# Triangular blocks through DRAM in 1 KB pieces on two queues, and more rotary and scaling work on GpSimd, in a two-layer hybrid backbone step

## The chip, the core and the metric

The kernel runs on one core of one Trainium2 chip. The time is device microseconds (us) of one execution. Three runs of the kernel before took 1982.02, 1990.4 and 2092.3 us, a median of 1990.4 us.

## The reference, cut to what matters

The program is one step of a two-layer backbone for 128 context tokens and 512 latent tokens, of width 1024. Every layer adds a gated mixer and a gated feed-forward to `x`. The mixer has four head groups side by side: grouped-query attention (GQA) with rotary, neighbourhood attention, a bidirectional gated delta rule (DeltaNet), and latent attention (MLA). The change touches three of them. For each of the 10 chunks of 64 tokens, both directions and 4 heads, DeltaNet solves a unit-triangular system:

```python
    a = jnp.where(strict, jnp.einsum('nbhid,nbhjd->nbhij', kb, kc) * dmask, 0.0)
    sol = lax.linalg.triangular_solve(a + jnp.eye(c, dtype=jnp.float32), rhs,
                                      left_side=True, lower=True, unit_diagonal=True)
    u, w = sol[..., :dv], sol[..., dv:]
    def step(s, xs):
        v_new = u_i - jnp.einsum('bhcd,bhde->bhce', w_i, s)
        ...
        s = s * gl_i[..., None, None] + jnp.einsum('bhcd,bhce->bhde', kd_i, v_new)
```

GQA normalises queries and keys per head and rotates them (`x1 * cos - x2 * sin`, `x2 * cos + x1 * sin`); MLA normalises its compressed query and key-value rows by a factor per token.

## The kernel before

All 640 tokens are worked on together, in fp32; a matrix product is made of three matmuls, from a rounded high part and the rest of each weight (`weights`, L311 to L322: a DMA load, a ScalarE cast into `whi`, a VectorE subtraction into `wlo`).

**The order on TensorE is written out by a planner.** `_Order` (L190 to L273) runs generators, each with a rank; a generator says with `yield` from which planned time on it may go on, and the first ready one of the lowest rank issues its matmuls next. `od.via(("DVE", 1.6), ...)` returns when a chain of operations on the named engines would be done by the planner's own bookkeeping, and `od.now + 9.5` is a plain delay. The order is fixed when the kernel is built: at run time TensorE takes its instructions in that order and waits where an operand is not there. The instructions of the other engines are put in order by a scheduler that simulates time, except those in `in_turn` (L303), which keep the order in which the program names them.

**The DeltaNet chain** (`delta_chain`, L785) has the rank 0 and runs through both layers' mixers: features, chunk matrices `M` (L988), inverse of 16x16 diagonal blocks (`inverse16`, L1014), two levels of doubling to 64x64 (`inverse`, L1061), the scan over chunks (L1159) and the output (L1246). Beside it the planner fills TensorE with projections (`rest`, L1901, dense, rank 2), and in the first layer with the modulation's products (`trickle`, L1930).

**`inverse16` makes two trips through DRAM.** The scratch `dinv` (L434) has for each of two trips the layout row group `r`, direction `d`, block `b` (20), quarter `q` (4), 256 elements. Trip 1: eight DMAs on SP (L1025) scatter the 16x16 blocks of `M` in 64-byte pieces, then two DMAs (L1034, L1035) of 160 KB each read them back, one block row of 4 KB to a partition, 40 partitions each; a VectorE copy (L1037, `in_turn`) transposes the second direction, and 60 small VectorE instructions per layer eliminate (L1044, L1048). Trip 2: two DMAs of 160 KB write the result (L1051, and L1052 behind the copy L1050), eight (L1055) gather it into `rt`, and VectorE's block transposes (L1081, `in_turn`) feed the first matmuls of `inverse` (`invp`). The planner allows 9.5 us for trip 1 and 10.0 us for trip 2.

In `inverse`, `fourth` copies the diagonal blocks of `rt` into `M` on VectorE (L1128, four copies for each of three groups); the scan's `ysp` matmuls read `M`. `gqa_norm` (L1409) scales `ar` on VectorE (L1425), multiplies by the gain on GpSimd (L1427), makes the sine part `gsw` on GpSimd (L1439), and does the last two operations of the rotary, times cosine and plus `gsw`, on VectorE (L1441, L1442), for four of five tiles. `mla_norm` (L1525) loads a tile of latent rows `mcr` (one buffer), rotates 32 columns on GpSimd, scales the other columns on VectorE (L1552, `in_turn`), and TensorE transposes it (`mtp`). GpSimd also makes `kd` (L1187) and the scaled state (L1191) for each step of the scan.

Of the kernel before, what the change touches and what calls it, by code (L numbers as in the profile page):

```python
# [11 lines left out]
F32 = mybir.dt.float32  # L12
# [3 lines left out]
ALU = mybir.AluOpType  # L16
# [11 lines left out]
L = 2  # L28
# [259 lines left out]
class _Build:  # L288
# [97 lines left out]
    def setup(self):  # L386
        nc, A, ctx = self.nc, self.A, self.ctx
        cp = self.cp = ctx.enter_context(self.tc.tile_pool(name="const", bufs=1))
        self.wp = ctx.enter_context(self.tc.tile_pool(name="wts", bufs=1))
        self.dp = ctx.enter_context(self.tc.tile_pool(name="dram", bufs=1, space=DRAM))  # L390
        cT = cp.tile([128, KD, 2], F32, name="cT")
        nc.sync.dma_start(out=cT, in_=A["cT"])
        pc = cp.tile([128, A["pcol"].shape[1]], F32, name="pcol")
        nc.sync.dma_start(out=pc, in_=A["pcol"])
        cb = cp.tile([128, A["cbase"].shape[1]], F32, name="cbase")
        nc.sync.dma_start(out=cb, in_=A["cbase"])
        cst = _constants()
        off = 0
        for k in _CBASE:
            n = cst[k].reshape(128, -1).shape[1]  # L400
            v = cb[:, off:off + n]
            off += n
            sh = cst[k].shape[1:]
            if len(sh) == 2:
                v = v.rearrange("p (a b) -> p a b", a=sh[0])
            elif len(sh) == 3:
                v = v.rearrange("p (a b c) -> p a b c", a=sh[0], b=sh[1])
            setattr(self, k, v)
        self.ones = cp.tile([128, 128], F32, name="ones")
        nc.vector.memset(self.ones, 1.0)  # L410
        par, off = {}, 0
        for k, sh in _PAR.items():
            n = int(np.prod(sh))
            v = pc[:, off:off + n]
            off += n
            if len(sh) == 2:
                v = v.rearrange("p (a b) -> p a b", a=sh[0])
            elif len(sh) == 3:
                v = v.rearrange("p (a b c) -> p a b c", a=sh[0], b=sh[1])
            par[k] = v  # L420
        self.par = par
        self.sc = cp.tile([128, KD, 32], F32, name="sc")
        nc.vector.memset(self.sc, 0.0)
        nc.scalar.activation(self.sc[:, :, 0:2], cT, AF.Silu)
        self.mods = [cp.tile([128, 48, 2], F32, name=f"mods{l}") for l in range(L)]
        self.oms = [cp.tile([128, 2, KD, 2], F32, name=f"oms{l}") for l in range(L)]
        self.dscr = {
            "x": self.dp.tile([128, KD, T], F32, name="dx"),
            "x1": self.dp.tile([128, KD, T], F32, name="dx1"),
            "nat": self.dp.tile([L, 4, 128, T], F32, name="dnat"),  # L430
            "bv": self.dp.tile([L, T, 256], F32, name="dbv"),
            "craw": self.dp.tile([L, 128, 5, 416], F32, name="dcraw"),
            "lat": self.dp.tile([L, 4, 128, T], F32, name="dlat"),
            "inv": self.dp.tile([L, 2, 2, 2, 20, 4, 256], F32, name="dinv"),  # L434
        }


# [438 lines left out]
    def gates(self, l, gz, dn, dt, ps):  # L876

        nc, od = self.nc, self.od
# [22 lines left out]
        nc.vector.tensor_tensor(out=ld, in0=m[:, 0], in1=eb, op=ALU.mult)  # L901
        self.lf = small("lf")
        nc.vector.tensor_scalar(out=self.lf, in0=m[:, 1], scalar1=-1.0, scalar2=None, op0=ALU.mult)
        yield od.via(("DVE", 1.6), ("ACT", 2.2), ("DVE", 0.5)) + 4.0
        yield "dn", 1
        gp = ps.tile([128, 2, 2, 10, 2], F32, tag="dn", name="gp")
        for d in range(2):
# [106 lines left out]
    def inverse16(self, l, dt):  # L1014

        nc, od = self.nc, self.od
        Z = self.dscr["inv"][l]
        rt = dt.tile([128, 2, 20, 32], F32, name="rt")
        nc.gpsimd.memset(rt.rearrange("p d b c -> p (d b c)"), 0.0)
        M = self.M.rearrange("p d n q c -> p d (n q) c")  # L1020

        for r in range(2):
            for q in range(4):
                p = slice(64 * r + 16 * q, 64 * r + 16 * q + 16)
                nc.sync.dma_start(out=Z[0, r, :, :, q].rearrange("d b (j i) -> j (d b) i", j=16),  # L1025
                                  in_=M[p, :, :, 16 * q:16 * q + 16].rearrange("p d b i -> p (d b) i"))

        def t(name):
            return self.ta(dt, name, 1024).rearrange("p (q j i) -> p q j i", q=4, j=16)

        X, V, W = t("ivx"), t("ivv"), t("ivw")
        S = W
        nc.gpsimd.memset(X.rearrange("p q j i -> p (q j i)"), 0.0)
        nc.sync.dma_start(out=X[0:40].rearrange("p q j i -> p (q j i)"), in_=Z[0, :, 0].rearrange("r b q e -> r b (q e)"))  # L1034
        nc.sync.dma_start(out=S[64:104].rearrange("p q j i -> p (q j i)"), in_=Z[0, :, 1].rearrange("r b q e -> r b (q e)"))  # L1035
        yield od.now + 9.5
        self.in_turn(nc.vector.tensor_copy(X[64:104], S[64:104].rearrange("p q j i -> p q i j")))  # L1037
        nc.gpsimd.tensor_copy(V.rearrange("p q j i -> p q (j i)"), self.eye16.unsqueeze(1).to_broadcast([128, 4, 256]))
        p = slice(0, 104)
        for j in range(15):  # L1040
            sh = [104, 2, j + 1, 15 - j]
            qs = (slice(0, 2), slice(2, 4))
            for q in qs:
                nc.vector.tensor_tensor(out=W[p, q, 0:j + 1, 0:15 - j], in0=V[p, q, 0:j + 1, j:j + 1].to_broadcast(sh),  # L1044
                                        in1=X[p, q, j:j + 1, j + 1:16].to_broadcast(sh), op=ALU.mult)
            for q in qs:
                v = V[p, q, 0:j + 1, j + 1:16]
                nc.vector.tensor_tensor(out=v, in0=v, in1=W[p, q, 0:j + 1, 0:15 - j], op=ALU.subtract)  # L1048
        yield od.via(("DVE", 18.0)) + 4.0
        nc.vector.tensor_copy(S[64:104], V[64:104].rearrange("p q j i -> p q i j"))  # L1050
        nc.sync.dma_start(out=Z[1, :, 0].rearrange("r b q e -> r b (q e)"), in_=V[0:40].rearrange("p q j i -> p (q j i)"))  # L1051
        nc.sync.dma_start(out=Z[1, :, 1].rearrange("r b q e -> r b (q e)"), in_=S[64:104].rearrange("p q j i -> p (q j i)"))  # L1052
        for r in range(2):
            for q in range(4):
                nc.sync.dma_start(out=rt[64 * r + 16 * q:64 * r + 16 * q + 16, :, :, 16 * (q % 2):16 * (q % 2) + 16]  # L1055
                                  .rearrange("p d b i -> p (d b) i"),
                                  in_=Z[1, r, :, :, q].rearrange("d b (j i) -> j (d b) i", j=16))
        yield od.now + 10.0
        return rt

    def inverse(self, rt, dt, ps):  # L1061
# [62 lines left out]
        def fourth(g, y):  # L1124
            a, b = groups[g]
            zp = bank(g)
            for q, p in enumerate(quads):
                nc.vector.tensor_copy(M[p, :, a:b, cols[q]], rt[p, :, a:b])  # L1128
            for d in range(2):
                for q in range(2):  # L1130
                    e, o = quads[2 * q + d], quads[2 * q + 1 - d]
                    for i in range(b - a):
                        self.mm(zp[e, d, i], y[o, d, i], rt[o, d, a + i])
            for d in range(2):
                for q in range(2):
                    e, o = quads[2 * q + d], quads[2 * q + 1 - d]
                    if q:
                        nc.scalar.mul(M[e, d, a:b, cols[1 - d]], zp[e, d], -1.0)
                    else:
                        nc.vector.tensor_scalar(out=M[e, d, a:b, cols[1 - d]], in0=zp[e, d], scalar1=-1.0, scalar2=None, op0=ALU.mult)  # L1140
# [268 lines left out]
    def gqa_norm(self, l, ar, dn, dt, ready):  # L1409
# [13 lines left out]
        for t in range(5):  # L1423
# [5 lines left out]
            if t < 4:  # L1429
# [7 lines left out]
                for b in range(2):  # L1437
                    for a in range(2):
                        nc.gpsimd.tensor_tensor(out=sv[:, :, a, b], in0=xv[:, :, a, 1 - b],  # L1439
                                                in1=sn[:, a, b].unsqueeze(1).to_broadcast([128, 6, 16]), op=ALU.mult)  # L1440
                nc.vector.tensor_tensor(out=x, in0=x, in1=cos.unsqueeze(1).to_broadcast([128, 6, 64]), op=ALU.mult)  # L1441
                nc.vector.tensor_tensor(out=x, in0=x, in1=sw.rearrange("p (h d) -> p h d", h=6), op=ALU.add)  # L1442
            yield od.via(("DVE", 1.5)) + 2.5

    def gqa_operands(self, l, g, ar, ma, at, ps):

# [78 lines left out]
    def mla_norm(self, l, dt, ps, S):  # L1525
# [7 lines left out]
        for t in range(5):  # L1533
# [13 lines left out]
                nc.gpsimd.tensor_tensor(out=x, in0=x, in1=sw, op=ALU.add)  # L1547
            else:
                nc.sync.dma_start(out=A["okr"][l], in_=cr[:, 384:416])
            yield od.now + 6.0  # L1550
            for q, (a, b) in enumerate(((0, 256), (256, 384))):
                self.in_turn(nc.vector.tensor_scalar(out=cr[:, a:b], in0=cr[:, a:b], scalar1=r[:, t, q:q + 1], scalar2=None,  # L1552
                                                     op0=ALU.mult))
            yield od.via(("DVE", 0.7)) + 2.0
            yield "w", 1
            tp = ps.tile([128, 4, 128], F32, tag="w", name="mtp")
            for f in range(4):
# [646 lines left out]
```

## Time and profile before

| | |
|---|---|
| runs | 1982.02, 1990.4, 2092.3 us; median 1990.4 us |
| profiled execution | 1986.23 us, span 1984.5 us |
| mean granted TensorE clock | 0.970 of full speed |
| busy share of the span | TensorE 93%, VectorE 55%, ScalarE 37%, GpSimd 14% |

The profiled execution is one run. PE is TensorE's matmuls, PEld its weight loads, DVE VectorE, ACT ScalarE, POOL GpSimd, SP the engine whose queue issues nearly all DMAs. Times in the rows are us from the start of the span; "[5.68 <-DMA ivw<-dinv]" behind a row is the idle time of the engine before it and what ended it. The first layer's mixer lies at 40 to 560 us, the second's at 1030 to 1500 us; the feed-forwards lie behind them.

### The profile page before, as it was taken

What the parts mean: (1) busy time and instruction counts of PE and PEld (TensorE: products, weight loads), DVE (VectorE), ACT (ScalarE), POOL (GpSimd) and SP (SyncE); (2) the same over time, 40 slices, a digit from 0 to 9 for tenths busy, and PEclk for the clock granted to TensorE, in tenths of its full rate; (3) what the DMA queues carried; (4) which work ended last, traced back from release to release, by engine and by line L of the source; (5) the groups of instructions that cost most, each with busy time, mean ns of one, the idle gap of its engine ahead of it and who ended that gap; (6) DMA issues with size and microseconds to landing.
All of it is one profiled execution on the core that took longest, in us unless ns stands there. A gap on an engine that the chain in (4) does not pass through costs nothing.

```text
span 1984.5 us, 40378 instructions
## 1 busy us (share of the span) xinstructions
PE 1855.4 (93%) x16620; PEld 1751.5 (88%) x16620; DVE 1098.1 (55%) x2372; ACT 734.1 (37%) x1505; POOL 282.7 (14%) x470
## 2 busy tenths in 40 slices
PE   5998998899999999999999889789999999999997
PEld 4976787778899999999989889677889999999997
DVE  6464646677657547647555674567765232333344
ACT  4622133766442212222345223277655221221231
POOL 1120312233310000000032131223322000000001
PEclk8998798999999999999999899899999999999999
DMA  7344333132535536435423222223352222222221
GB/s 295 128 114 122 112 94 104 30 108 73 165 130 167 158 99 191 150 113 188 131 89 109 57 76 70 74 56 75 90 172 80 77 78 79 75 67 83 74 96 54
DMA packets 116521, 213.51 MB, mean 108 GB/s; under 512 B 44401, under 2 KB 64369, under 8 KB 116209
## 3 DMA queue, kind: packets, MB, share of 16 engines
q1 hardware_dynamic: 113520, 206.22, 33.3%
q0 software_dynamic: 2816, 4.72, 1.2%
q8 instruction: 130, 2.13, 0.4%
q14 instruction: 55, 0.44, 0.1%
HBM read 186.29 MB, written 19.89 MB: 104 GB/s over the span
## 4 chain that ended last, share of the span: by engine, by line
PE 77%; DVE 8%; DMA 6%; ACT 4%; issue 2%; SPq 2%; POOL 1%; DVEq 0%; ACTq 0%; POOLq 0%
PE acc L351 56%; PE tacc L351 7%; PE ptp L363 2%; PE sc L351 2%; PE pvo L351 2%; PE invp L351 1%; DVE wlo L309 1%; DMA wst<-wout 1%; PE mpart L351 1%; DMA ivw<-dinv 1%; ACT p L1288 1%; ACT whi L308 1%; PE ysp L351 1%; PE spp L351 1%; SPq L1705 1%
## 5 line engine op out<-in xcount | busy, mean ns | idle before, releaser
L351 PE MATMUL acc<-h,whi 128*128 128x256 f32 (+1 forms) x3520 | 685.0, 313 | 2.6 <-ACT h L574 1.4
L351 PEld LDWEIGHTS acc<-h,whi 128*128 128x128 f32 x3520 | 582.6, 190 | 12.4 <-issue 5.1
L308 ACT CAST whi<-wst 128x1024 fp32r<-128x1024 f32 (+3 forms) x210 | 203.6, 970 | 714.6 <-PE acc L351 664.9
L351 PE MATMUL acc<-h,wlo 128*128 128x256 f32 (+1 forms) x1760 | 414.7, 313 | 7.7 <-DVE wlo L309 7.7
L309 DVE TENSOR_TENSOR wlo<-wst,whi 128x1024 fp32r<-128x1024 f32 (+3 forms) x210 | 237.8, 1133 | 210.7 <-ACT whi L308 209.8
L351 PEld LDWEIGHTS acc<-h,wlo 128*128 128x128 f32 x1760 | 322.6, 191 | 10.8 <-DVE wlo L309 8.8
L351 PE MATMUL acc<-g,whi 128*128 128x256 f32 (+1 forms) x1128 | 216.6, 309 | 0.0
L351 PEld LDWEIGHTS acc<-g,whi 128*128 128x128 f32 x1128 | 185.9, 188 | 0.1
L541 POOL TENSOR_TENSOR sq<-sq 128x256 f32<-128x256 f32 (+1 forms) x48 | 48.6, 1012 | 926.2 <-ACT sq L535 925.8
L1806 DVE SCALAR_TENSOR_TENSOR x<-acc,mods,x 128x256 f32<-128x256 f32 (+1 forms) x144 | 55.6, 434 | 186.5 <-PE acc L351 186.4
L507 DVE SCALAR_TENSOR_TENSOR wmj<-wmd,cb 128x1024 f32<-128x1024 f32 x112 | 136.8, 1221 | 39.6 <-DMA wmd<-wmodT 38.4
L351 PE MATMUL tacc<-whi,h 128*128 128x256 f32 (+1 forms) x640 | 149.3, 316 | 1.5 <-ACT whi L308 1.5
L351 PE MATMUL acc<-g,wlo 128*128 128x384 f32 (+1 forms) x564 | 135.2, 309 | 0.0
L351 PEld LDWEIGHTS tacc<-whi,h 128*128 128x128 f32 x640 | 111.5, 195 | 10.5 <-issue 5.0
L351 PE MATMUL acc<-oh,whi 128*128 128x384 f32 (+1 forms) x512 | 115.1, 315 | 1.9 <-DVE xe L1806 1.9
L363 PE MATMUL ptp<-cbase,p 128*128 128x128 f32 x512 | 81.4, 284 | 29.6 <-ACT p L1288 12.3
L351 PEld LDWEIGHTS acc<-g,wlo 128*128 128x128 f32 x564 | 103.2, 188 | 0.0
L351 PE MATMUL tacc<-wlo,h 128*128 128x256 f32 (+1 forms) x320 | 98.9, 309 | 1.8 <-DVE wlo L309 1.8
L363 PEld LDWEIGHTS ptp<-cbase,p 128*128 128x128 f32 x512 | 57.0, 142 | 45.9 <-ACT p L1288 17.1
L2122 DVE TENSOR_TENSOR sg<-acc,sg 128x256 f32<-128x256 f32 x88 | 39.1, 485 | 101.9 <-PE acc L351 101.9
L1288 ACT ACTIVATE p<-sc,sm 128x768 f32<-128x768 f32 (+1 forms) x96 | 79.8, 831 | 33.4 <-DVE sm L1285 23.9
L351 PEld LDWEIGHTS acc<-oh,whi 128*128 128x128 f32 x512 | 84.7, 190 | 4.5 <-PE acc L351 2.4
(322 smaller groups left out, 2624.8 us busy)
## 6 DMA issues: line engine op xcount, KB each, us to landing
wmd<-wmodT SPq DMA_DIRECT2D x56, 512.0 KB, 4.3
wst<-wg SPq DMA_DIRECT2D x44, 512.0 KB, 3.6
wst<-wu SPq DMA_DIRECT2D x44, 512.0 KB, 3.6
wmd<-wmod SPq DMA_DIRECT2D x40, 512.0 KB, 6.6
wst<-wd SPq DMA_DIRECT2D x34, 448.0 KB, 3.7
wst<-wfm SPq DMA_DIRECT2D x24, 512.0 KB, 4.8
wst<-wd SPq DMA_DIRECT2D x16, 512.0 KB, 4.2
wst<-wout SPq DMA_DIRECT2D x28, 256.0 KB, 3.1
```

What stands on the lines that cost most here:

```text
L308: self.nc.scalar.copy(hi, src)
L309: self.nc.vector.tensor_tensor(out=lo, in0=src, in1=hi.bitcast(F32), op=ALU.subtract)
L351: self.nc.tensor.matmul(out, lhsT, rhs, start=start, stop=stop)
L363: self.nc.tensor.transpose(out, in_, self.ident)
L507: nc.vector.scalar_tensor_tensor(out=j, in0=st, scalar=1.0, in1=self.cb[:, g], op0=ALU.mult, op1=ALU.mult, accum_out=self.msum[:, e, g:g + 1])
L541: (eng or nc.gpsimd).tensor_tensor(out=self.sq[hf][0], in0=self.sq[hf][0], in1=sq, op=ALU.add)
L1288: nc.scalar.activation(p, s, AF.Exp, bias=m, accum_out=d)
L1705: nc.sync.dma_start(out=u[16 * r:16 * r + 16, j], in_=ap)
L1806: self.nc.vector.scalar_tensor_tensor(out=x_out[:, a:b], in0=o[h][:, a - HB * h:b - HB * h], scalar=m[:, 8 * gate + e, grp:grp + 1], in1=x ...
L2122: nc.vector.tensor_tensor(out=sg[:, s], in0=ou[q], in1=sg[:, s], op=ALU.mult)
```

## The change

The scratch gets the quarter as its outer dimension, so that a partition's 4 KB lie in four pieces of 1 KB. The scatter of trip 1 goes out on two queues, four DMAs from SP and four from ScalarE. The read of trip 1 and the write of trip 2 are four DMAs of 80 KB each, by direction and row group, instead of two of 160 KB. The copies into `M` (L1128), the last two rotary operations (L1441, L1442) and the scaling of the latent rows (L1552, no longer `in_turn`) go from VectorE to GpSimd. Five delays that the planner works with are changed.

```diff
-            "inv": self.dp.tile([L, 2, 2, 2, 20, 4, 256], F32, name="dinv"),
+            "inv": self.dp.tile([L, 2, 4, 2, 2, 20, 256], F32, name="dinv"),
...
-        yield od.via(("DVE", 1.6), ("ACT", 2.2), ("DVE", 0.5)) + 4.0
+        yield od.via(("DVE", 1.6), ("ACT", 2.2), ("DVE", 0.5)) + 2.0
...
-        for r in range(2):
+        for r, eng in enumerate((nc.sync, nc.scalar)):
             for q in range(4):
                 p = slice(64 * r + 16 * q, 64 * r + 16 * q + 16)
-                nc.sync.dma_start(out=Z[0, r, :, :, q].rearrange("d b (j i) -> j (d b) i", j=16),
-                                  in_=M[p, :, :, 16 * q:16 * q + 16].rearrange("p d b i -> p (d b) i"))
+                eng.dma_start(out=Z[0, q, r].rearrange("d b (j i) -> j (d b) i", j=16),
+                              in_=M[p, :, :, 16 * q:16 * q + 16].rearrange("p d b i -> p (d b) i"))
...
-        nc.sync.dma_start(out=X[0:40].rearrange("p q j i -> p (q j i)"), in_=Z[0, :, 0].rearrange("r b q e -> r b (q e)"))
-        nc.sync.dma_start(out=S[64:104].rearrange("p q j i -> p (q j i)"), in_=Z[0, :, 1].rearrange("r b q e -> r b (q e)"))
-        yield od.now + 9.5
+        def rows(t, d, r):
+            return t[64 * d + 20 * r:64 * d + 20 * r + 20].rearrange("p q j i -> p q (j i)")
+        for d, t in enumerate((X, S)):
+            for r in range(2):
+                nc.sync.dma_start(out=rows(t, d, r), in_=Z[0, :, r, d].rearrange("q b e -> b q e"))
+        yield od.now + 8.0
...
-        nc.sync.dma_start(out=Z[1, :, 0].rearrange("r b q e -> r b (q e)"), in_=V[0:40].rearrange("p q j i -> p (q j i)"))
-        nc.sync.dma_start(out=Z[1, :, 1].rearrange("r b q e -> r b (q e)"), in_=S[64:104].rearrange("p q j i -> p (q j i)"))
+        for d, t in enumerate((V, S)):
+            for r in range(2):
+                nc.sync.dma_start(out=Z[1, :, r, d].rearrange("q b e -> b q e"), in_=rows(t, d, r))
...
-                                  in_=Z[1, r, :, :, q].rearrange("d b (j i) -> j (d b) i", j=16))
-        yield od.now + 10.0
+                                  in_=Z[1, q, r].rearrange("d b (j i) -> j (d b) i", j=16))
+        yield od.now + 8.0
...
-                nc.vector.tensor_copy(M[p, :, a:b, cols[q]], rt[p, :, a:b])
+                nc.gpsimd.tensor_copy(M[p, :, a:b, cols[q]], rt[p, :, a:b])
...
-                nc.vector.tensor_tensor(out=x, in0=x, in1=cos.unsqueeze(1).to_broadcast([128, 6, 64]), op=ALU.mult)
-                nc.vector.tensor_tensor(out=x, in0=x, in1=sw.rearrange("p (h d) -> p h d", h=6), op=ALU.add)
-            yield od.via(("DVE", 1.5)) + 2.5
+                nc.gpsimd.tensor_tensor(out=x, in0=x, in1=cos.unsqueeze(1).to_broadcast([128, 6, 64]), op=ALU.mult)
+                nc.gpsimd.tensor_tensor(out=x, in0=x, in1=sw.rearrange("p (h d) -> p h d", h=6), op=ALU.add)
+            yield od.via(("DVE", 0.8), ("Pool", 5.5 if t < 4 else 1.5))
...
-            yield od.now + 6.0
             for q, (a, b) in enumerate(((0, 256), (256, 384))):
-                self.in_turn(nc.vector.tensor_scalar(out=cr[:, a:b], in0=cr[:, a:b], scalar1=r[:, t, q:q + 1], scalar2=None,
-                                                     op0=ALU.mult))
-            yield od.via(("DVE", 0.7)) + 2.0
+                nc.gpsimd.tensor_scalar(out=cr[:, a:b], in0=cr[:, a:b], scalar1=r[:, t, q:q + 1], scalar2=None, op0=ALU.mult)
+            yield od.now + 9.0
```

## Rows read from the trace of the kernel before

**Rows 1.** The page: busy us, share of the span, instructions of each engine.
```profile
PE 1855.4 (93%) x16620; PEld 1751.5 (88%) x16620; DVE 1098.1 (55%) x2372; ACT 734.1 (37%) x1505; POOL 282.7 (14%) x470
```

**Rows 2.** Stretches: width, TensorE busy (instructions), granted clock, DMA share, GB/s.
```profile
130.00:134.70 4.70, 0.39 (x3) 1.00 0.11 44
134.70:142.00 7.30, 7.30 (x35) 0.54 0.41 144
168.90:172.40 3.50, 0.17 (x9) 1.00 0.14 47
172.40:186.00 13.60, 9.55 (x169) 0.51 0.55 116
223.50:226.50 3.00, 0.00 (x0) 1.00 0.72 235
226.50:247.00 20.50, 20.47 (x275) 0.52 0.17 53
1114.00:1120.20 6.20, 0.02 (x1) 0.84 0.01 6
1120.20:1128.50 8.30, 8.26 (x33) 0.50 0.19 63
1171.50:1179.00 7.50, 2.60 (x74) 0.82 0.11 26
1265.00:1293.00 28.00, 14.88 (x280) 0.68 0.20 60
```

**Rows 3.** The chain of waits in order of time, first layer: start, us, what.
```profile
123.08 8.96 DMA ivw<-dinv
...
162.91 8.15 DMA dinv<-ivw
...
174.79 3.20 DMA rt<-dinv
```

**Rows 4.** The SP queue's timeline, second layer's trip 1: start, us, instruction.
```profile
1099.90 4.22 SPq L1025 DMA_DIRECT2D dinv<-dM  x8
```

**Rows 5.** One us of trip 1's read: width, clock, DMA share, GB/s.
```profile
1110.00:1111.00 1.00, 1.00 0.13 53
```

**Rows 6.** VectorE's timeline: start, us, instruction, shapes, idle before and its end.
```profile
132.14 1.03 DVE L1037 COPY ivx<-ivw 40x1024 f32<-40x1024 f32 x1 [5.68 <-DMA ivw<-dinv]
...
224.17 0.55 DVE L1552 TENSOR_SCALAR mcr<-mcr,mrs 128x256 f32<-128x256 f32 x2 [1.30 <-DMA mcr<-dcraw]
...
1115.62 1.02 DVE L1037 COPY ivx<-ivw 40x1024 f32<-40x1024 f32 x1 [8.11 <-DMA ivw<-dinv]
...
1175.21 0.56 DVE L1441 TENSOR_TENSOR ar<-ar,gsw 128x384 f32<-128x384 f32 x1 [0.62 <-POOL gsw L1439]
...
1177.76 0.49 DVE L1081 STREAM_TRANSPOSE ivr<-rt 128x128 f32<-128x128 f32 x2
```

**Rows 7.** TensorE's timeline: the inverse's matmuls behind the block transposes.
```profile
226.53 2.49 PE L351 MATMUL invp<-ivr,dM 32*32 32x32 f32 x64 [3.04 <-DVE ivr L1081]
```

**Rows 8.** GpSimd's groups by shape: count, busy us, mean ns, idle before.
```profile
L1291 POOL TENSOR_SCALAR dg<-cbase,sd 128x128 f32<-128x128 f32 x96 | 58.5, 610 | 185.9 <-DVE sd L1289 146.4 <-issue 12.4 <-PE sc L351 9.3
L541 POOL TENSOR_TENSOR sq<-sq 128x384 f32<-128x384 f32 x24 | 26.7, 1111 | 464.5 <-ACT sq L535 464.5
...
L755 POOL COPY qk<-convin 128x640 f32<-128x640 f32 x4 | 3.2, 799 | 24.5 <-ACT convin L751 24.5
```

**Rows 9.** Lines moved from VectorE: count, ns min/median/max, first and last start.
```profile
L1128 DVE COPY dM<-rt x24: 240/417/654, 202.3 to 1193.8; 32x512 f32<-32x512 f32 x16, 32x256 f32<-32x256 f32 x8
...
L1441 DVE TENSOR_TENSOR ar<-ar,gsw x8: 557/592/1073, 214.1 to 1178.8; 128x384 f32<-128x384 f32 x8
```

**Rows 10.** GpSimd from inverse to scan, both layers: width, busy (instructions), granted clock, DMA.
```profile
180.00:240.00 60.00, 16.83 (x30) 0.81 0.39 116
1160.00:1220.00 60.00, 18.53 (x38) 0.94 0.26 78
```

**Rows 11.** ScalarE's timeline behind the place of trip 1's scatter.
```profile
119.93 1.05 ACT L308 CAST whi<-wst 128x1024 fp32r<-128x1024 f32 x1 [7.91 <-PE acc L351]
```

## The prediction

> **What bounds the kernel now.** First I read the busy shares of the page: TensorE is busy 1855.4 us, 93% of the span, with its weight loads beside it, and no other engine reaches 60% [rows 1]. So a change that adds or removes no matmul can only give back time in which TensorE stands idle or runs at half clock. Then I split the two mixers into short stretches and looked where that time lies [rows 2]. For a stretch, the loss is width minus busy, plus busy times (1 - clock), the clock as a share of its upper level. [...]
>
> [...] B0, trip 2: 3.3 idle, then 13.6 us with 9.55 busy at 0.51, loss 4.05 + 4.7: 12.1 us. C0, the second half of the inverse: 3.0 idle, then 20.5 us at 0.52, loss 9.8: 12.8 us. A1, second layer, trip 1: 6.2 idle, then 8.3 us at 0.50, loss 4.1: 10.3 us. B1, first half of the inverse: 7.5 us with 2.6 busy at 0.82, 5.4 us. [...] Each time the clock falls behind an idle TensorE and stays low for some us of work.
>
> Who makes it idle? [...] VectorE stood in front of the `in_turn` copy L1037 for 5.68 us in the first layer and 8.11 in the second, with the next weight's subtraction `wlo` behind it [rows 6], and TensorE ran out of weights. During the read only 0.13 of the 16 DMA engines is busy, which is two engines, at 53 GB/s [rows 5]: 320 KB at that pace are 6 us. C0 has another cause: VectorE's transposes stand behind L1552, which waited 1.30 us for `mcr` [rows 6], and `invp` waited 3.04 us for them [rows 7]. At B1 a transpose at 1177.76 stands behind rotary operations that wait for GpSimd's `gsw` [rows 6].
>
> **The change part by part.** *Trip 1.* Eight issues take 4.22 us on SP, 0.53 each [rows 4]; four on each of two queues are 2.1, so 2.1 us less, or nothing if the DMA engines and not the issues set the pace. The read becomes four DMAs. No row shows 1 KB pieces over 20 partitions. The nearest small DMA of this scratch, the gather, lands 3.20 us behind its issue although its pieces are 64 bytes [rows 3]: three more issues and that are 3 x 0.53 + 3.2 = 4.8 us, against 0.53 + 8.96 = 9.5 now, 4.7 less. At the other end the pieces stay on two engines: 8.96 and two more issues, 1.1 us more than now. I take 4.7, because the block row of 20 is the outer dimension where a pair was, and the two busy engines match the pair. [...] So L1037 runs 6.8 us earlier (2.1 if only the two queues work, 1.1 later if nothing does). VectorE's 5.68 us of waiting goes in the first layer, 6.8 of 8.11 in the second. What is late next is ScalarE's cast and the weight load itself, which keep pace elsewhere. I recover 7 of A0's 7.7 and 9 of A1's 10.3.
>
> The four DMAs issued by ScalarE hold its queue 2.1 us, in front of a cast that has 7.91 us of idle time ahead of it [rows 11]: nothing; without that cover 2.1 us a layer. SP issues four scatters less and four others more, two for each trip: nothing. SP's later weight loads wait behind its reads as now, only shorter.
>
> *Trip 2.* The first two writes go during the copy L1050, so the write costs 2 x 0.53 + 3.2 = 4.3 us against 8.15 + 0.53 now: 4.4 less, or 1.1 more at the other end. The modulation load behind it no longer shares its engines. But the planner now puts the first `invp` 2 us earlier in the order (8.0 for 10.0), and the trip still takes 1.1 (copy) + 4.3 + 8 x 0.53 + 3.2, less one issue, 12.3 us. So part of the wait stays: of B0's 12.1 I recover 6 (2 to 11).
>
> *Rotary and scaling leave VectorE.* The transposes no longer stand behind L1552 or L1441. In the second layer B1's 5.4 us go: 5. In the first, the 3.0 us idle goes; half of the slow 20.5 us comes from that idle time and half from the thin 32x32 matmuls themselves, my estimate, so 3 + 4: 7 of 12.8 (3 to 12). VectorE also loses 24 block copies of 0.417 us, 10 us, and 16 rotary operations of about 0.59, 9.5 us [rows 9].
>
> *GpSimd gains it.* Per layer: eight rotary operations of 128x384 at 1.11 us [rows 8], 8.9; five scalings of 128x256 and five of 128x128, the latter 0.61 [rows 8] and the former at most twice that, 9.2; eight copies of 512 columns at 0.64 (0.8 for 640 [rows 8]) and four of 256 at 0.32, 6.4. That is 24.5 us beside the 16.8 and 18.5 us that it does in the 60 us where most falls [rows 10]: 41 to 43 of 60, room, but in order. `mtp` on TensorE and the scan's `ysp` now wait for GpSimd. Between nothing and the 6.4 us of copies per layer I take 3. And VectorE slows where GpSimd works: L1441 took 0.557 to 1.073 us [rows 9]. With about 30 new GpSimd instructions per layer, half meeting VectorE at 0.5 us each and a quarter of that on the path, 2 us. Together 10 us in two layers (4 to 17).
>
> *Due times.* Gates 2 us, trip 1 1.5, trip 2 2.0 earlier in the order, GQA tiles 2.4 us later each (0.8 + 5.5 for 1.5 + 2.5, and one hand-over), MLA tiles as before (6.0 + 0.6 + 0.7 + 0.15 + 2.0 = 9.45, now 9.0). TensorE's order changes in both mixers; I count zero, with 10 us either way for the range.
>
> **The sum.** 7 + 6 + 7 + 9 + 5 = 34 us back, 10 us new, 24 net. The profiled execution took 1986.2 us (span 1984.5), 4.2 below the median of the runs: 1986.2 - 24 = **1962 us**, 1.4% under the median.
>
> **The rivals.** *The waits come back behind the inverse* (0.20). The fill-in work is the same, and in the second layer it is gone near 1265: there 28 us hold only 14.9 busy [rows 2], with the scan's own latency left. The chain shortens by 6.8 + 4.4 = 11.2 us a layer, TensorE gains 20 in the first and 14 in the second; the difference, 9 + 3, is lost again at the end of the scan, and 2 more at low clock: 1976 us. For it: the tail. Against it: C0 and B1 shorten the chain too.
>
> *GpSimd's queue becomes the chain* (0.09, the slow side). The place is the start of the scan: block copies and `kd` stand in GpSimd's order behind the rotary. It decides from the point where GpSimd's last L1128 ends later than VectorE's last L1140. If half of the 24.5 us is exposed in each layer and half as much again lost to the clock, 18 x 2 = 36 us replace the 6 I charged, and C0 and B1 do not come back, 12: 1962 + 30 + 12 = 2004 us. For it: GpSimd's rotary can't start before VectorE's scaling, so its new work can't be spread forward. Against it: 17 to 19 us of 60 used now [rows 10].
>
> *VectorE is held by GpSimd* (0.10). If each of 15 meetings a layer costs the whole GpSimd instruction, 1.1 us, and half of that is on the path, 8 us a layer replace 2: 1974 us. [...]
>
> *The trips do not get shorter* (0.05): 1 KB pieces on the same two engines. A0, B0 and A1 stay, 22 us, and eight issues more, 4: 1962 + 22 + 4 = 1988 us.
>
> *More comes back* (0.09): B0 and C0 in full, 12 us, and a part of the tail's 13 us of idle time through the earlier order, 8: 1942 us.
>
> **How the numbers follow.** The forecast, 1948 to 1976, has 0.47. From 1942 to 2004 the cases spread on both sides; the range 1940 to 1990 leaves out the GpSimd queue's upper part and some of the last case, under 2 in 10. Two per cent, about what a measurement of this kernel can tell from no change, are 40 us: below 1947 lie the last case and the lower edge of the forecast, 0.13; above 2026 the worst of the GpSimd queue, 0.03; within, 0.84.
>
> **What would show it.** In the new trace, VectorE's wait in front of L1037 under 2 us in both layers and a DMA share well above 0.13 in the reads; no half clock behind 134 and 1120; `invp` of the second layer never waiting 4.9 us for a transpose; GpSimd at 41 to 43 us where it had 17 to 19, with its last L1128 copy done before the scan's first `ysp`. It is wrong if TensorE's idle and slow time in the two mixers falls by less than 10 us or more than 45, or if `mtp` or `ysp` wait for GpSimd over 5 us at a time.

## The result and the profile after

The changed kernel takes 1965.9 us (median of five runs, 1963.4 to 1969.9); the kernel before took 1989.9 us on the same chip (median of five, 1978.6 to 2092.3). The run of 2092.3 us lies in a slower state and is left out of the ratio. The ratio is 0.9898, 95% interval [0.9872, 0.9924]. On another chip, beside the last experiments, it was 0.992 [0.9894, 0.9945]. So the change is worth about 1%, or 16 to 20 us; the forecast was 1962 us, 24 less than the profiled execution of before. The profiled execution took 1966.6 us (span 1964.6), 19.7 less than that of before. A second profiled execution had a span of 1974.5 us: one profile places a gain only to within some 10 us, so single stretches are read for their mechanism and the ratios for the size.

First the page: busy us, share of the span, instructions of each engine. It answers to [rows 1].

```profile
PE 1850.0 (94%) x16620; PEld 1745.2 (89%) x16620; DVE 1080.8 (55%) x2312; ACT 734.6 (37%) x1505; POOL 333.3 (17%) x530
```

VectorE lost 17 us and GpSimd gained 50.6, 25.3 a layer where 24.5 was forecast. How far each layer moved is read from one operation of the feed-forward behind each mixer; the two groups show its count, ns, first and last start. First the kernel before, over the span and in the second layer alone:

```profile
L2122 DVE TENSOR_TENSOR sg<-acc,sg x88: 414/485/550, 560.8 to 1920.8; 128x256 f32<-128x256 f32 x44, 128x384 f32<-128x384 f32 x44
...
L2122 DVE TENSOR_TENSOR sg<-acc,sg x44: 415/486/550, 1512.8 to 1920.8; 128x256 f32<-128x256 f32 x22, 128x384 f32<-128x384 f32 x22
```

The same operation in the changed kernel:

```profile
L2126 DVE TENSOR_TENSOR sg<-acc,sg x88: 412/486/552, 551.1 to 1900.3; 128x256 f32<-128x256 f32 x44, 128x384 f32<-128x384 f32 x44
...
L2126 DVE TENSOR_TENSOR sg<-acc,sg x44: 415/486/552, 1492.7 to 1900.3; 128x256 f32<-128x256 f32 x22, 128x384 f32<-128x384 f32 x22
```

The first layer gained 560.8 - 551.1 = 9.7 us, the second (1512.8 - 1492.7) - 9.7 = 10.4. The forecast had 15 (7 + 6 + 7, less 5 of new costs) and 9 (9 + 5, less 5). In the second profiled execution of the changed kernel (e12) the same two readings give 4.5 and 5.8. So the first layer fell short, by 5 to 10 us; the second lies between 3 under the forecast and 1 over it. The stretches of TensorE that answer to [rows 2] say where (width, busy, granted clock, DMA share, GB/s):

```profile
130.00:134.70 4.70, 4.70 (x37) 1.00 0.31 111
134.70:142.00 7.30, 7.30 (x52) 1.00 0.17 49
145.00:151.20 6.20, 0.00 (x0) 0.86 0.82 243
151.20:165.00 13.80, 12.70 (x93) 0.57 0.55 114
165.00:168.70 3.70, 1.32 (x35) 1.00 0.76 163
168.70:177.00 8.30, 8.26 (x92) 0.79 0.25 71
197.00:210.00 13.00, 8.89 (x161) 0.64 0.34 118
210.00:247.00 37.00, 37.00 (x682) 0.99 0.44 133
1090.00:1128.50 38.50, 38.22 (x336) 1.00 0.40 105
1128.50:1172.00 43.50, 40.08 (x1080) 1.00 0.30 75
1172.00:1181.00 9.00, 9.00 (x168) 0.62 0.01 2
```

The rows at 130 to 142 are full and at the upper clock: A0's 7.7 us (the first layer's trip 1: 4.3 idle, then 3.4 lost in 7.3 us at 0.54 [rows 2]) are gone. So are A1's 10.3, but for 0.3 (1090 to 1128.5). But the stretch from 145.0 to 177.0 now loses 6.2 idle, then 1.1 + 12.70 x 0.43 = 6.6, then 2.4, then 8.26 x 0.21 and 0.04 = 1.8: 17.0 us where B0 lost 12.1. C0's successor (197 to 247) loses 4.1 + 3.2 + 0.4 = 7.7 instead of 12.8. The first layer's places together give 7.7 - 4.9 + 5.1 = 7.9 back, the second's A1 10.0. That is 17.9 of the 20. The windows are only roughly the same work, so two legs between events, in the first layer: from VectorE's copy behind trip 1 to the first `invp` 46.6 us (132.14 to 178.71) became 52.9 (124.17 to 177.11), and from there to the first `ysp` 76.9 became 67.3. The loss lies between the trips, the gain in the inverse.

What stands at 145? The chain of waits there (start, us, what):

```profile
143.62 0.44 PE mtp L363 x4
...
144.09 2.46 DMA mcr<-dcraw
...
146.72 5.01 POOL mcr L1557 x2
151.73 0.38 POOL msw L1551 x2
```

TensorE transposes the first tile of latent rows (`mtp`), whose scalings ran at 93 us, and the second tile is due right behind it. The rows have one buffer, so the second load starts only then, 2.5 us, and the two scalings on GpSimd take 5.0 us. TensorE waits 6.2 us in one piece, of which GpSimd has the rows for the last 4.5. Behind it the granted clock is 0.50 until 160.0 us and 0.69 from there to 165.0. In the second profile the same wait is 3.3 + 3.1 us. TensorE's row, and GpSimd's for the third tile, whose pair takes 1.5 us with VectorE busy for 0.08 of them:

```profile
151.20 1.05 PE L363 MATMUL mtp<-cbase,mcr 128*128 128x128 f32 x3 [6.23 <-POOL mcr L1557]
...
156.53 1.50 POOL L1557 TENSOR_SCALAR mcr<-mcr,mrs 128x256 f32<-128x256 f32 x2 [3.77 <-DMA mcr<-dcraw]
```

In the kernel before, the first `mtp` ran at 217.4 us; now it runs at 143.5.

The trip itself, in the second layer. The SP queue (start, us, instruction), then VectorE's copy behind the read:

```profile
1087.28 2.22 SPq L1025 DMA_DIRECT2D dinv<-dM  x4
1092.72 0.28 SPq L1040 DMA_DIRECT2D ivx<-dinv  x1
1093.10 0.28 SPq L1040 DMA_DIRECT2D ivw<-dinv  x1
1093.48 0.28 SPq L1040 DMA_DIRECT2D ivx<-dinv  x1
1093.81 0.33 SPq L1040 DMA_DIRECT2D ivw<-dinv  x1
```

```profile
124.17 1.08 DVE L1042 COPY ivx<-ivw 40x1024 f32<-40x1024 f32 x1 [0.87 <-DMA ivw<-dinv]
...
1097.26 1.13 DVE L1042 COPY ivx<-ivw 40x1024 f32<-40x1024 f32 x1 [2.42 <-DMA ivw<-dinv]
```

From the first scatter to the copy it is 1097.26 - 1087.28 = 10.0 us, before 1115.62 - 1099.90 = 15.7 [rows 4, 6]. VectorE's waits of 5.68 and 8.11 us are 0.87 and 2.42 (under 2 was forecast for both). The chain has the last legs:

```profile
1088.82 3.71 DMA dinv<-dM
...
1093.81 3.38 DMA ivw<-dinv
```

### The profile page after: what moved, and what is told of

Same layout as the page of the kernel before. It is cut to its first block, busy times and chain, and to the rows that moved or that the text cites. A ratio compares the mean times of both kernels' runs of the same rounds, so it can differ in the third digit from the quotient of the medians.

```text
span 1964.6 us, 40383 instructions
## 1 busy us (share of the span) xinstructions
PE 1850.0 (94%) x16620; PEld 1745.2 (89%) x16620; DVE 1080.8 (55%) x2312; ACT 734.6 (37%) x1505; POOL 333.3 (17%) x530
## 4 chain that ended last, share of the span: by engine, by line
PE 79%; DVE 9%; DMA 4%; ACT 4%; issue 2%; SPq 1%; POOL 0%; DVEq 0%; ACTq 0%; POOLq 0%
PE acc L351 57%; PE tacc L351 6%; PE pvo L351 3%; PE ptp L363 3%; PE sc L351 2%; PE invp L351 1%; PE mpart L351 1%; DVE wlo L309 1%; ACT p L1294 1%; DMA wst<-wout 1%; ACT whi L308 1%; DMA wmd<-wmod 1%; PE ysp L351 1%; ACT pt L1329 1%; DVE nq L1770 1%
## 5 line engine op out<-in xcount | busy, mean ns | idle before, releaser
L351 PE MATMUL acc<-h,wlo 128*128 128x256 f32 (+1 forms) x1760 | 410.5, 310 | 0.8 <-DVE wlo L309 0.8
L309 DVE TENSOR_TENSOR wlo<-wst,whi 128x1024 fp32r<-128x1024 f32 (+3 forms) x210 | 242.0, 1154 | 202.0 <-ACT whi L308 197.1
L351 PEld LDWEIGHTS tacc<-whi,h 128*128 128x128 f32 x640 | 111.0, 193 | 12.3 <-issue 6.3
L1297 POOL TENSOR_SCALAR dg<-cbase,sd 128x128 f32<-128x128 f32 x96 | 58.5, 610 | 206.4 <-DVE sd L1295 147.1
```

The lines of the kernel that those rows point to most:

```text
L309: self.nc.vector.tensor_tensor(out=lo, in0=src, in1=hi.bitcast(F32), op=ALU.subtract)
L351: self.nc.tensor.matmul(out, lhsT, rhs, start=start, stop=stop)
L1297: nc.gpsimd.tensor_scalar(out=dg, in0=self.ident, scalar1=d, scalar2=None, op0=ALU.mult)
```

## The experiments

My theory T: the shorter trips make the gain, the moves to GpSimd give about as much as they take, and what they take is the `mtp` wait. Each kernel was timed beside the kernel before; the ratios are to it. The first four ran on one chip, and so did the next four and the last four.

**The trips alone** (e1: `fourth`, `gqa_norm` and `mla_norm` as before).

```
-   nc.gpsimd.tensor_copy(M[p, :, a:b, cols[q]], rt[p, :, a:b])
+   nc.vector.tensor_copy(M[p, :, a:b, cols[q]], rt[p, :, a:b])
...
```

> Only the trips and the due times that belong to them (scratch layout, two queues, reads and writes of 1 KB pieces, 2.0/8.0/8.0); rotary, scaling of the latent rows and block copies stay on VectorE as before. Theory T (the waits of the two trips made the gain, and the moves to GpSimd give about as much as they take): 1965 to 1972 us, the whole gain of the change within 4 us, with TensorE full at 115 to 145 us and at 1090 to 1135 us, and no stall of mtp behind GpSimd near 146 us. Rival M (the moves to GpSimd made half of the gain or more): 1976 to 1985 us. Rival S (the trips alone are worth more, and the moves cost): 1955 to 1963 us.

1971.9 us, 0.9896 [0.987, 0.9921]: as T said, the whole gain is here already, that of the trips with their due times. TensorE is busy 29.4 of the 30 us from 115 at the upper clock, and no `mtp` waits. But 145 to 165 us holds only 12.27 busy all the same; there it waits for the modulation's load `wmd`, 7.4 us in two waits.

**The moves alone** (e2: the old scratch, queues and trips; `fourth`, `gqa_norm`, `mla_norm` as changed).

> Only the moves to GpSimd (rotary, scaling of the latent rows, block copies) with their due times; both trips as before. Theory T: 1983 to 1992 us, no gain outside the spread, with the idle times of TensorE near 130 and 1114 us still there (4 to 6 us each, half clock behind). Rival M: 1970 to 1978 us. Rival S: 1994 to 2002 us.

1982.1 us, 0.995 [0.9927, 0.9974]. All three theories missed: the moves bring some 10 us on the old trips and, by the first experiment, about nothing on the new ones. The idle place at 130 us is still there (0.61 busy of 4.70). The scalings have the new delay of 9.0 here too, but the second tile's `mtp` runs at 218.2 us, and in the first layer none waits for GpSimd.

**Scaling back on VectorE** (e3).

```
+   yield od.now + 6.0
-       nc.gpsimd.tensor_scalar(out=cr[:, a:b], ...)
-   yield od.now + 9.0
+       self.in_turn(nc.vector.tensor_scalar(out=cr[:, a:b], ...))
+   yield od.via(("DVE", 0.7)) + 2.0
```

> The changed kernel with the scaling of the latent rows on VectorE in program order with its two old delays. Theory T (the pair of scalings takes 5 us on GpSimd beside VectorE's elimination, and TensorE's mtp stands behind it): the idle time of TensorE at 145 to 152 us and the slow clock behind it are gone, 7 to 12 us, but C0's wait of the block transposes behind the scaling comes back, 3 to 7: 1957 to 1965 us. Rival D (mtp waits for the load of its rows, and GpSimd only passes that on): the same stall of 5 us or more before the first mtp, 1966 to 1972 us.

1962.5 us, 0.9847 [0.9821, 0.9872]: T. No `mtp` stands at 145 us, its first one is at 243.2. The other half of T missed: from 177 to 260 us no `invp` waits for a block transpose, so C0's wait did not come back. What is late next there is the modulation's load. TensorE's waits of 140 to 172 us (us in total, times, longest):

```profile
PE mpart L351 <- DMA wmd<-wmod: 7.1, 2, 3.8
```

**Block copies back on VectorE** (e4: the reverse of the one line L1134).

> The changed kernel with the block copies of the inverse back on VectorE. Theory T (off the path on either engine: GpSimd has room, VectorE is not the bound there): 1963 to 1969 us. Rival Q (the copies on GpSimd stand in front of the scan's first operands): 1957 to 1962 us. Rival V (VectorE between the inverse's groups was the path): 1971 to 1977 us.

1976.0 us, 0.9921 [0.9892, 0.9949]. Rival Q fell; T and V can't be told apart beside 0.9898 and 0.992 of the changed kernel. What the copies are worth can't be told from the noise.

**`mtp` later in the order, scaling still on GpSimd** (e5).

```
-   yield od.now + 9.0
+   yield od.now + 14.0
```

> The changed kernel with the latent rows' transposes (mtp) planned 14.0 us behind their load and scaling instead of 9.0; the scaling stays on GpSimd. Theory O (the order put mtp on TensorE before the pair of scalings, slowed beside VectorE's elimination, could be ready): no mtp waits over 1 us for GpSimd at 140 to 165 us, and the time is like that with the scaling on VectorE, 0.983 to 0.987 of before. Rival G (the scaling on GpSimd is too slow wherever it stands, and later mtp only shift the wait or delay the latent rows): 0.988 to 0.992.

1963.0 us, 0.9869 [0.9846, 0.9892], inside O's range, though its interval meets the changed kernel's. The first tile's `mtp` stays at 143.3 us; the second's, 5 us later in its delay, moves from 151.2 to 235.7. The second pair of scalings still takes 4.0 us, but nobody waits. GpSimd's timeline of this kernel:

```profile
146.60 3.99 POOL L1557 TENSOR_SCALAR mcr<-mcr,mrs 128x256 f32<-128x256 f32 x2 [9.76 <-DMA mcr<-dcraw]
```

No `mtp` waits between 140 and 172 us; again `wmd` does, 6.1 us.

**Scaling on ScalarE** (e6).

```
+   yield od.now + 6.0
-       nc.gpsimd.tensor_scalar(out=cr[:, a:b], ...)
-   yield od.now + 9.0
+       nc.scalar.mul(cr[:, a:b], cr[:, a:b], r[:, t, q:q + 1])
+   yield od.via(("ACT", 0.9)) + 2.0
```

> The changed kernel with the scaling of the latent rows on ScalarE, planned at the old delays (6.0, then 0.9 + 2.0). Theory O: no mtp behind GpSimd, and no block transpose behind the scaling either, so as fast as with the scaling on VectorE or up to 4 us faster, 0.982 to 0.986 of before. Rival A (ScalarE's queue stands behind the load of the rows, and with it the casts of the weights): 0.988 to 0.993.

1964.1 us, 0.9866 [0.9845, 0.9887], between the two. The `mtp` wait is gone, but ScalarE stood 15.5 us, in six waits, for the load of the rows, which is rival A's mechanism. Three ways of taking the scaling out of TensorE's way give 0.985 to 0.987.

**Old 4 KB pieces, but DMAs of 20 partitions** (e7).

```
-   Z [L, 2, 4, 2, 2, 20, 256];  in_=Z[0, :, r, d].rearrange("q b e -> b q e")
+   Z [L, 2, 2, 2, 20, 4, 256];  in_=Z[0, r, d].rearrange("b q e -> b (q e)")
```

> The changed kernel with the old layout of the scratch (4 KB pieces), each direction still written and read as two DMAs of 20 partitions. Theory E (the two busy engines came from the pair as the outer dimension; 20 as the outer dimension spreads over more): the read lands 3 to 4.5 us behind its issue as in the changed kernel, with a DMA share of 0.5 or more, and the time is that of the changed kernel within 4 us, 0.988 to 0.992. Rival P (it is the 1 KB pieces): the read lands 6 to 9 us behind its issue, and the time is 6 to 12 us above that of the changed kernel, 0.993 to 0.996.

1965.7 us, 0.988 [0.9859, 0.9901]. From the first read's issue to the copy it takes 4.3 us in the second layer (1091.91 to 1096.17), 4.5 in the changed kernel. So it is not the 1 KB pieces; the trace fits theory E. Two windows of 1 us during this read (width, busy of PE, PEld, DVE, ACT, POOL, clock, DMA share, GB/s), beside 0.13 and 53 GB/s before [rows 5]:

```profile
1093.00:1094.00 1.00, 1.00 (x9) 1.00 (x8) 1.00 (x2) 0.00 (x0) 0.00 (x0) 1.00 0.60 197
1094.00:1095.00 1.00, 1.00 (x9) 1.00 (x8) 0.05 (x1) 0.00 (x0) 0.00 (x0) 1.00 0.80 193
```

**All eight scatters on SP** (e8).

```
-   for r, eng in enumerate((nc.sync, nc.scalar)):
+   for r, eng in enumerate((nc.sync, nc.sync)):
```

> The changed kernel with all eight scatters of trip 1 on SP. Theory I (the issues set the pace of the scatter): its last DMA and the read behind it come 1.5 to 2.5 us later in each layer, TensorE still has work there, and the time rises by 0 to 3 us: 0.990 to 0.992 of before. Rival N (the DMA engines set the pace): no leg moves by more than 0.5 us and the time stays at 0.989 to 0.991. Rival W (SP's weight loads behind four more issues come late): 0.993 to 0.997.

1971.1 us, 0.9901 [0.9878, 0.9924]: the time fits I and N alike, but the legs did move, and the other way. The SP queue of the second layer, one queue:

```profile
1088.47 4.22 SPq L1025 DMA_DIRECT2D dinv<-dM  x8
1092.86 0.32 SPq L1040 DMA_DIRECT2D ivx<-dinv  x1
1093.28 0.28 SPq L1040 DMA_DIRECT2D ivw<-dinv  x1
1094.34 0.27 SPq L1040 DMA_DIRECT2D ivx<-dinv  x1
1094.66 0.33 SPq L1040 DMA_DIRECT2D ivw<-dinv  x1
```

The first two reads, of row group 0, go out while the scatter of row group 1 is still landing; with two queues both groups land together and all four reads wait. From the first scatter to the copy it takes 8.5 us (1088.47 to 1096.95) against 10.0, and 10.0 against 11.8 in the first layer. The second queue makes the trip longer; in the time of the kernel that can't be seen.

**Only the planner's delays, in the kernel before** (e9: 2.0, 8.0 and 8.0 for 4.0, 9.5 and 10.0).

> The kernel before with only the three shorter delays of the planner (gates 2.0 for 4.0, trip 1 8.0 for 9.5, trip 2 8.0 for 10.0). Theory T (the waits' length decides; what is planned earlier only waits longer): 0.997 to 1.003 of before, the read of trip 1 still 8 to 9 us. Rival R (the new order makes the gain): 0.990 to 0.994.

2001.1 us, 1.0065 [1.0047, 1.0083]: slower by 13 us, outside both theories. TensorE's waits from 110 to 345 us:

```profile
PE mpart L351 <- DMA wmd<-wmod: 13.8, 4, 9.8
PE ssp L351 <- ACT convy L757: 3.9, 1, 3.9
PE invp L351 <- issue: 3.3, 1, 3.3
```

In the kernel before, `wmd` had 4.9 us there and `ssp` none. TensorE's order puts work ahead of data that isn't there.

**Trips and copies as changed, rotary and scaling on VectorE** (e10: e3 with L1447, L1448 and their delay as before).

> The trips as changed and the block copies on GpSimd; rotary and scaling on VectorE as before. Theory H (rotary on VectorE stands in front of the inverse's transposes while it waits for GpSimd, and the copies matter less): 0.988 to 0.991 of before, near the trips alone (0.9896). Rival C (the copies on GpSimd carry the gain that the version with scaling on VectorE has over the trips alone): 0.984 to 0.987.

1965.0 us, 0.9894 [0.9874, 0.9913]: H. It equals the trips alone, so the rotary carries what e3 has over them, some 9 us; the two intervals just miss each other. Behind it stands B1's old wait; TensorE's waits from 1130 to 1230 us:

```profile
PE invp L351 <- DVE ivr L1087: 5.8, 2, 5.4
```

With the rotary on GpSimd (e3), the same wait:

```profile
PE invp L351 <- issue: 3.4, 3, 1.7
PE invp L351 <- DVE ivr L1087: 0.5, 2, 0.3
```

**A better version: scaling on VectorE and one queue** (e11: the edits of e3 and e8), and **the changed kernel again** beside it (e12).

> The changed kernel with the scaling of the latent rows on VectorE and all eight scatters of trip 1 on SP. If the two halves of the read that can start behind their own half of the scatter are worth more than the second queue (as the legs with one queue say, 1.5 to 1.8 us a layer), and no mtp stands behind GpSimd: 0.981 to 0.985 of before, 8 to 17 us under the changed kernel. Rival: the 1.5 us are lost again at the next wait, the modulation's load: 0.985 to 0.988.

> The changed kernel itself once more, on the same chip as the three others: 0.987 to 0.992 of before by all theories; it is there so that the version with the scaling on VectorE is compared with it directly.

e11 takes 1955.3 us, 0.9838 [0.9822, 0.9854]; e12, on the same chip, 1972.1, 0.992 [0.9894, 0.9945]. The version is 17 us faster than the change and beats both kernels; the expected range held. Beside e3's 0.9847 the one queue can't be told from nothing, so most of the gain over the change is the scaling's. Its stretches of TensorE:

```profile
130.00:142.00 12.00, 12.00 (x87) 1.00 0.15 56
145.00:165.00 20.00, 14.52 (x141) 0.74 0.59 134
165.00:177.00 12.00, 10.77 (x234) 0.86 0.34 98
1090.00:1128.50 38.50, 38.50 (x367) 1.00 0.39 90
```

145 to 177 us loses 5.5 + 3.8 + 1.2 + 1.5 = 12.0 us instead of 17.0. In the 12 that stay, TensorE's longest waits are for the modulation's load, 5.8 us in two; it has one buffer, and a second wasn't tried.

## Why the prediction was right, and where it was not

*Trip 1* was right in its sum: from the first scatter to the copy it takes 6.4 us less in the first layer and 5.7 in the second, for 6.8. Inside it, the read was right: 9.65 us from its first issue to its landing became 4.5, so 5.2 less for 4.7. Its reason, the outer dimension of 20, fits: 4 KB pieces do the same (e7, 4.3 us), and the DMA share in the read is 0.60 and 0.80 there, 0.57 and 0.73 in the changed kernel (1094 to 1096 us) and 0.13 before, other loads included. But the read also became four DMAs instead of two, and no run tells the two apart: that the outer dimension does it was my estimate. The last read lands 3.4 us behind its issue, 3.2 in the sum. The second queue was mis-sized: 2.1 us forecast, and the scatter lands 5.25 us behind its first issue for 5.85, 0.6 less, while the overlap of the halves is lost (e8, 1.5 to 1.8 us). SP's issues take 2.22 us for 4.22, and of these 2.0 us the landing shows only 0.6.

*A0 and A1*: 7.7 and 10.0 us back for 7 and 9. VectorE's wait in front of the copy was the cause in both, but "TensorE ran out of weights" holds for A1 alone. In A0 a product of the modulation stood there, held by VectorE behind the copy. The kernel before:

```profile
134.70 0.64 PE L351 MATMUL mpart<-wmd,sc 128*32 128x256 f32 x8 [4.31 <-DVE ivw L1044]
...
1120.24 0.90 PE L351 MATMUL acc<-h,wlo 128*128 128x256 f32 x2 [6.22 <-DVE wlo L309]
```

*Trip 2* took what was forecast: from the copy at 155.10 to the first transpose at 167.54 it is 12.4 us, 12.3 by the sum. But B0 gave nothing back, where 6 was forecast. The first `invp` started on TensorE at 177.1, 9.6 us after that transpose began: it no longer waited for its operands, but for its turn. Two steps of the prediction failed here.

The first is that the term for B0 has no wait for the modulation's load, of which it says only that it "no longer shares its engines". The load did get shorter: it takes 3.79 us from issue to landing, where before, beside the write, it took 8.7 (issued at 163.59, its product waited until 172.35). Which DMA engines the two shared, no view shows. But it has one buffer, and in the changed kernel SP issues it behind the eight gathers of trip 2, which wait for the write. Its buffer had its last reader at 159.74 to 160.82, and the load goes out at 164.91. The SP queue of the changed kernel, then of the kernel before, where the load went out ahead of the gathers:

```profile
160.68 4.13 SPq L1061 DMA_DIRECT2D rt<-dinv  x8
164.91 15.51 SPq L449 DMA_DIRECT2D wmd<-wmod  x4
...
163.59 0.94 SPq L449 DMA_DIRECT2D wmd<-wmod  x1
171.12 4.17 SPq L1055 DMA_DIRECT2D rt<-dinv  x8
```

So trip 2 still stands in the chain of waits: the write, the gathers' issues, then the load, for which TensorE waits 2.4 us. It has little else to do: in the kernel before it was busy 23.2 of the 23.7 us from 145. That this is the work which now fills A0 is likely, but no run shows it. In the versions without the `mtp` wait (e1, e3, e5, e6, e10, e11) the leg from the copy behind trip 1 to the first `invp` is still 48.7 to 51.0 us, before 46.6. No run moved this load ahead of the gathers, so its part alone is not shown.

The second is the sentence on due times, "MLA tiles as before (6.0 + 0.6 + 0.7 + 0.15 + 2.0 = 9.45, now 9.0)". The old path went through VectorE's planned time, and the first `mtp` stood at 217 us. The new 9.0 goes through no engine; with the short trips it puts the first `mtp` at 143.5 and the second right behind it, ahead of a pair of scalings that takes 5.0 us there. I had added up the delay of one tile and not asked where it lands. e5 changes the order alone and the wait is gone. Kernels with this wait (the changed one twice, e4, e7, e8) take 51.6 to 58.8 us for the same leg.

*The due times* were counted at zero, ten either way. Three of the five alone cost 13 us (e9). What they are worth inside the change wasn't separated.

*Rotary* was right: B1's `invp` waits at most 0.6 us for a transpose (1.3 in the second profile), 4.9 in the kernel before and 5.4 in e10. From the second layer's first transpose to its first `ysp` it is 55.8 us (57.6), 62.8 before and 61.4 in e10. C0 gave 5.1 for 7.

*The sum* came out nearer than its terms. B0 missed by 11 us. Of the 10 us charged for GpSimd's new work, only the `mtp` wait shows among TensorE's waits for GpSimd, and it is part of B0's loss already. That the two nearly cancel is luck.

*GpSimd's durations* came out near: rotary 1.006 us (1.11 forecast), copies 0.632 and 0.504 (0.64, 0.32), the 128x256 scaling 1.696 (at most 1.2). The mean of the last hides its spread: its pair with the 128x128 one takes 1.5 us where VectorE is mostly idle and 5.0 to 5.8 beside the elimination. The forecast of 41 to 43 us in [rows 10]'s stretches was wrong, 24.1 and 22.2: the scaling, no longer behind VectorE's order, starts at 93 us, and the second layer's work lies earlier (35.7 us from 1130 to 1190). No `ysp` waited for GpSimd: its last copy runs at 1170.8, the second layer's first `ysp` at 1189.4.

*The rivals.* That the waits come back is true between the trips: with the read no longer late, TensorE runs out of ready work and waits for the modulation's load in every version with short trips (e1, e3, e5, e11). At the tail too: the second layer's first `ysp` starts 31.2 us earlier (1220.6 to 1189.4) and its last `otp` 27.0 (1293.0 to 1266.0), of which 20.1 arrive at the feed-forward. GpSimd's queue became the chain at one point only, the `mtp` wait, 6.2 us at a time. Over 5 us was one of the prediction's own signs of being wrong, and at this place it was. VectorE was slow beside GpSimd only in places: during the block copies at 197.3 to 200.0 us three of its six smallest two-input operations take 0.59 to 0.63 us, the other three 0.18 to 0.19, and all of them 0.17 to 0.19 right behind the copies. That each meeting costs VectorE the whole 1.1 us of a GpSimd instruction, the term in that rival's sum, no run shows: these three lose some 0.4 us each, the other three nothing. The second layer's elimination, from copy to copy, takes 25.0 us, 25.1 before.

## What to carry to other kernels

A transfer that feeds an in-order engine is worth shortening: as four DMAs with 20 as the outer dimension instead of two with a pair, the read landed in 4.5 us instead of 9.65. The halves of a scatter in series let each half's read start early (e8: 8.5 us from scatter to copy, 10.0 with the halves side by side). When an operation changes engine, look at which engines its due time went through: without the old one, its reader is planned earlier, here to a place where the new engine took 5.0 us for a pair that takes 1.5 elsewhere. Gains of two edits need not add: the moves to GpSimd brought some 10 us on the long trips and about nothing on the short ones, where their reader met a slow scaling. And look what stands in a queue behind a round trip: here a load with a free buffer went out 4 us late.

## What the hardware showed that I had not expected

A pair of scalings on GpSimd took up to 3.8 times as long (5.75 us for 1.50) beside VectorE's two-operand work. GpSimd's timeline of the changed kernel in the second layer:

```profile
1116.42 5.75 POOL L1557 TENSOR_SCALAR mcr<-mcr,mrs 128x256 f32<-128x256 f32 x2 [9.84 <-DMA mcr<-dcraw]
```

The pair takes 5.75 us while VectorE runs the elimination and the convolution back to back, busy for all of them; in the first layer it takes 5.0, with VectorE busy for 4.0. That VectorE is busy doesn't settle it: at 1134.5 us the pair takes 1.50 with VectorE busy throughout (block transposes, reductions and `dQ`), and in e7 and e8 it takes 2.4 and 2.7 us where it took 5.0 in the changed kernel. What decides between these is open. The slow one was GpSimd at 146 and 1116 us, and VectorE at 197 (0.59 to 0.63 us for 0.17 to 0.19). In the second layer, eight scatters over two queues land only 0.6 us sooner than over one, 5.25 us behind the first issue for 5.85.
